# Hybrid decoder layer on one core: the conditioning vector and the first channels' vectors as 11 rows in a transfer of their own

## Chip, cores and metric

The kernel runs on one core of a Trainium2 chip. The metric is the device time of one execution in microseconds (us); lower is better. The time before is the median of three runs.

## What is computed

One decoder layer over 512 tokens and 1024 channels. A conditioning vector `c` yields a shift, a scale and a gate; the normalised input is modulated by shift and scale and goes through one input projection, whose columns feed an attention group and a recurrent group; both are gated, joined and projected back, and a last RMS norm closes the layer. Only the opening concerns the change:

```python
c_act = jax.nn.silu(c)
mod = c_act @ w_mod[l] + b_mod[l]
shift, scale, gate = jnp.split(mod, 3, axis=-1)
h = rmsnorm(x, norm_gain[l]) * (1.0 + scale[:, None, :]) + shift[:, None, :]
proj = h @ w_in[l]
q, k, v, z_attn, x_lru, z_lru = jnp.split(proj, splits, axis=-1)
# attention and RG-LRU groups, each RMS-normed and gated by silu(z)
x = x + gate[:, None, :] * y          # y: both groups through w_out
return rmsnorm(x, final_gain)
```

All of it is in float32.

## The kernel before

Channels lie on the 128 partitions, in eight blocks `d` = 0 to 7 of 128 channels; tokens lie in four tiles `t` of 128. TensorE (PE) computes the products, VectorE (DVE) the sums over weights and the low halves of split operands, ScalarE (ACT) the activations and the high halves; the queue of SyncE (SP) issues nearly all loads. Large products are done three times with operands split into a high and a low part (`split`, line 246), so that they keep float32 accuracy.

**Order of the work.** Every operation is handed to a planner (`Plan`, line 61) with its engine, an assumed cost and a due time. `emit` (line 97) simulates the engines and buffers with these assumed numbers and writes each engine's instructions in the order so found. A changed cost, due time or dependency can therefore move instructions anywhere, and each engine then works through its own list strictly in order.

**The opening.** One table of vectors, `vec` (128 partitions x 80 columns: gains, biases, `c` and others), is loaded from ACT's queue (line 274) beside the four tiles of `x`, which SP loads (line 275). POOL builds the identity matrix `ident`. Then:

- ACT takes silu of the eight columns of `c` into `ccol` (line 317), then loads the table for square roots (line 318). For each token tile it computes the sum of squares and its root (lines 339 and 340), then scales the first 256 channels of tiles 2 and 3 into `xs` (line 348). DVE does that for tiles 0 and 1 (line 351).
- PE spreads `ccol` over all partitions: eight transposes of a column broadcast to 128 x 128, four into each bank `cp` (line 326). DVE copies them into `cb` (line 233).
- DVE multiplies the modulation weights `ws` with `cb` and sums along the row, one sum per channel (line 375 for block 0, line 387 for the others). Then it adds the biases and multiplies by the gain: `g` holds a block's shift (column 0) and its scale (column 1).
- PE turns a block's 128 channels of all four tiles into the bank `xp` (line 407 for block 0, line 403 for the others). ACT makes `h` from `xp` and `g` (line 410), once rounded (`h0h` for block 0) and once in full; DVE subtracts them for the low part. Then PE sums the products of the first seven column blocks into the banks `acc` (line 422).
- Ahead of all that PE has 31 matmuls of 512 columns on a constant tile, `spare` (line 309, `NWARM`), whose result nobody reads. They stand in PE's list between the transposes, where the planner puts them.

After block 7 the rest of the projection, attention, recurrence and output follow, with `vec` read at many places; `spt` (lines 433 to 447) is a small chain on POOL, DVE and ACT that prepares the recurrence's decay, and `halves` (line 476) is half of 20 columns of `vec`.

Of the kernel before, what the change touches and what calls it, by code (L numbers as in the profile page):

```python
# [10 lines left out]
AF = mybir.ActivationFunctionType  # L11
OP = mybir.AluOpType
# [5 lines left out]
ND = D // 128  # L18
# [8 lines left out]
V_GAIN, V_SHIFT, V_SCALE, V_GATE = 0, 8, 16, 24  # L27
V_CW, V_CB, V_BR, V_BI, V_LAM, V_AG, V_LG = 32, 48, 52, 56, 60, 64, 68
V_C = 72
# [31 lines left out]
class Plan:  # L61
# [11 lines left out]
    def op(self, eng, cost, fn, r=(), w=(), due=None, table=None, lat=0.25, after=0.0, alt=None):  # L73
        o = Op(eng, cost, fn, list(r), list(w), due, table, lat, after, alt)
        deps = set()
        for b in o.r:
            if b.writer is not None:
                deps.add(b.writer)
        for b in o.w:
            if b.writer is not None:  # L80
                deps.add(b.writer)
            deps.update(b.readers)
        for b in o.r:
            b.readers.append(o)
        for b in o.w:
            b.writer, b.readers = o, []
        for b in set(o.r) | set(o.w):
            b.users += 1
        deps.discard(o)
        o.deps = list(deps)  # L90
        for d in deps:
            d.outs.append(o)
        o.left = len(deps)
        self.ops.append(o)
        return o
# [80 lines left out]

@with_exitstack
def tile_hymba_block(ctx: ExitStack, tc: tile.TileContext, x, ws0, wss, wgt, win0, wv, winr,
                     wo, wg, vecs, fgain, consts, out):
    nc = tc.nc  # L180
    V, A, G, PE, SP = nc.vector, nc.scalar, nc.gpsimd, nc.tensor, nc.sync
    N2, N4, N8 = 37, 18, 5
# [17 lines left out]
    op = plan.op  # L200
# [4 lines left out]
    def t4(name, dt=F32, shape=(128, 1024)):  # L205
        return Buf("t4", list(shape), dt, name)

    def bank(name, kind=None):
        return Buf("ps", [128, 512], F32, name, kind)

    def col(name):
        return Buf("c", [128, 2], F32, name)

    def fix(name, shape, dt=F32):
        return Buf("fix", list(shape), dt, name)


    def dv(n, ptr=0):
        return 0.075 + n / 960.0 + 0.06 * ptr
# [10 lines left out]
    def copy(n, dst, src, r, w, due=None, psum=False, after=0.0):  # L230

        op("A", acp(n) if psum else ac(n), lambda: A.copy(dst(), src()), r, w, due, after=after,  # L232
           alt=("V", dv(n) if psum else dv2(n), lambda: V.tensor_copy(dst(), src())))
# [4 lines left out]
    def load(dst, src, due, kb=512, queue=SP):  # L238
        op("SP", kb / 390.0, lambda: queue.dma_start(dst[:], src), [], [dst], due, lat=1.9 if due < -98.9 else 2.4 if due < T_REST - 8 else 3.3)
# [21 lines left out]
    def t_first(d):  # L261
        return T_FIRST + 4.79 * d
# [8 lines left out]

    xt = [t4(f"x{t}") for t in range(NT)]
    vec, ident, cst = fix("vec", [128, NV]), fix("ident", [128, 128]), fix("cst", [128, 2048])
    op("A", 0.45, lambda: A.dma_start(vec[:], vecs), [], [vec], -30, lat=1.5)
    for t in range(NT):
        load(xt[t], x[t * 128:(t + 1) * 128, :], -99 + 0.3 * t)
    ws, w0 = {}, {}
    for d in range(ND):
        if d == 0:
            ws[d] = [[Buf("t4" if up - lo > 512 else "t2", [128, up - lo], F32, f"ws0{j}{n}") for n, (lo, up) in enumerate(CUTS[j])] for j in range(2)]  # L280
            for j in (1, 0):
                for n, (lo, up) in enumerate(CUTS[j]):
                    at = 128 * (1024 * j + lo)
                    load(ws[d][j][n], ws0[at:at + 128 * (up - lo)].rearrange("(p n) -> p n", p=128), -97.2 + 0.2 * n - 0.5 * j,
                         kb=(up - lo) / 2)
            w0[d] = [Buf("t2", [128, n], F32, f"w00{n}") for n in (512, 384)]
            load(w0[d][0], win0[d][:, 0:512], -96, kb=256)
            load(w0[d][1], win0[d][:, 512:896], -95, kb=192)
            continue
        w0[d] = t4(f"w0_{d}", F32, (128, 128 * NFIRST))  # L290
        if d < 4:
            ws[d] = [t4(f"ws{d}{j}") for j in range(2)]
            for j in (1, 0):
                load(ws[d][j], wss[d, j], -90 + 3 * (d - 1) - j)
        else:
            b = Buf("t8", [128, 2, 1024], F32, f"ws{d}")
            load(b, wss[d].rearrange("j p n -> p j n"), t_first(d) - 9, kb=1024)
            ws[d] = [b, b]
        load(w0[d], win0[d], t_first(d) - 8.9 if d >= 4 else -92 + 3 * d, kb=448)
# [10 lines left out]
           [warm], [spare], 5.3 + 0.28 * n, lat=0.0)  # L310


    epsc, ones, junk, ccol = fix("epsc", [128, 1]), fix("ones", [128, 1]), fix("junk", [128, 1]), fix("ccol", [128, ND])
    op("V", 0.1, lambda: V.memset(epsc[:], EPS), [], [epsc], -20)
    op("V", 0.1, lambda: V.memset(ones[:], 1.0), [], [ones], 0)
    op("A", 0.1, lambda: A.activation(junk[:], epsc[:], AF.Silu), [epsc], [junk], -6, "silu")
    op("A", 0.1, lambda: A.activation(ccol[:], vec[:, V_C:V_C + ND], AF.Silu), [vec, junk], [ccol], -5, "silu")
    op("A", 0.1, lambda: A.activation(junk[:], epsc[:], AF.Sqrt), [epsc, ccol], [junk], -4, "sqrt")
    cb = t4("cb")
    for half in range(2):  # L320
        ps = bank("cp")
        s = slice(half * 512, (half + 1) * 512)

        def spread(ps=ps, half=half):
            for j in range(4):
                PE.transpose(ps[:, j * 128:(j + 1) * 128], ccol[:, half * 4 + j:half * 4 + j + 1].to_broadcast([128, 128]),  # L326
                             ident[:])
        op("PE", 0.6, spread, [ccol, ident], [ps], 2)
        copy(512, lambda s=s: cb[:, s], lambda ps=ps: ps[:], [ps], [cb], 4.5 + 0.5 * half, True)


# [3 lines left out]
    for t in range(NT):  # L335
# [8 lines left out]
        for dst, cut, e, due2, after in ((xs[t], slice(0, 256), "VVAA"[t], due + 0.4, 0.0), (xt[t], slice(256, D), "A", 20.0 + t, REST[t])):  # L344
            o = (lambda d_, c_: d_[:] if d_ in xs else d_[:, c_])
            n = cut.stop - cut.start
# [3 lines left out]
            else:  # L350
# [6 lines left out]
    hl = [t2(f"h{d}l", F32R) for d in range(ND)]  # L357
    acc = [bank(f"acc{j}") for j in range(NFIRST)]
    op("V", 0.1, lambda: V.tensor_scalar(vec[:, V_SCALE:V_SCALE + ND], vec[:, V_SCALE:V_SCALE + ND], 1.0, None,
                                         op0=OP.add), [vec], [vec], -3)  # L360

    sch = col("sch")

    def part(d, j):
        return ws[d][j][:, j] if d >= 4 else ws[d][j][:]

    def gain(d):

        sc, g = col("sc"), col("g")
        half = (sc, sch)  # L370
        for j in (1, 0):
            if d == 0:
                for n in range(2):
                    lo, up = CUTS[j][n]
                    op("V", dv(up - lo), lambda j=j, n=n, lo=lo, up=up: V.scalar_tensor_tensor(
                        ws[0][j][n][:], ws[0][j][n][:], 1.0, cb[:, lo:up], op0=OP.mult, op1=OP.mult,
                        accum_out=half[n][:, j:j + 1]), [ws[0][j][n], cb], [ws[0][j][n], half[n]], 8 - 2 * j + 0.7 * n)
                    if not n:
                        op("V", 0.1, lambda j=j, v=(V_SHIFT, V_SCALE)[j]: V.tensor_add(
                            sc[:, j:j + 1], sc[:, j:j + 1], vec[:, v:v + 1]), [sc, vec], [sc], 9.2)  # L380
                if j:
                    op("V", 0.2, lambda: V.tensor_scalar(g[:, 1:2], sch[:, 1:2], sc[:, 1:2], vec[:, V_GAIN:V_GAIN + 1],
                                                         op0=OP.add, op1=OP.mult), [sc, sch, vec], [g], 9.4)
                else:
                    op("V", 0.1, lambda: V.tensor_add(g[:, 0:1], sch[:, 0:1], sc[:, 0:1]), [sc, sch], [g], 9.5)
                continue
            op("V", dv(1024), lambda j=j: V.scalar_tensor_tensor(  # L387
                part(d, j), part(d, j), 1.0, cb[:], op0=OP.mult, op1=OP.mult, accum_out=sc[:, j:j + 1]),
               [ws[d][j], cb], [ws[d][j], sc])
        if d == 0:  # L390
            return g
        op("V", 0.2, lambda: V.tensor_scalar(
            g[:, 1:2], sc[:, 1:2], vec[:, V_SCALE + d:V_SCALE + d + 1], vec[:, V_GAIN + d:V_GAIN + d + 1],
            op0=OP.add, op1=OP.mult), [sc, vec], [g])
        op("V", 0.1, lambda: V.tensor_add(g[:, 0:1], sc[:, 0:1], vec[:, V_SHIFT + d:V_SHIFT + d + 1]), [sc, vec], [g])
        return g

    for d in range(ND):
        g, xp = gain(d), bank(f"xp{d}")
# [18 lines left out]
        for i, (a, b) in enumerate(((0, hh[d]), (1, hh[d]), (0, hl[d]))):  # L418
            for j in range(NFIRST):
                w, k = wp[j // 4][a], j if d else j % 4  # L420
# [288 lines left out]
    for u, name in enumerate(UNITS):  # L709
        kind, idx = name[0], int(name[1])  # L710
        t1 = t_step(8 * (u + 1))
        ps = unit(u)
# [41 lines left out]
    for g in range(4):  # L754
        br, half = "la"[g // 2], g % 2
# [5 lines left out]
        for j in range(2):  # L761
            w = t4(f"wo{g}{j}", F32, (128, 2, 512))
# [4 lines left out]
        for t in range(NT):  # L767
# [3 lines left out]
            for n, (lo, up) in enumerate(zip(cuts, cuts[1:])):  # L771
                ps, w = bank("po"), up - lo
# [39 lines left out]
                for to, up, mark in ((outa[t], 512, done_a), (outb[t], 512, done_b))[:1 if last else 2]:  # L812
                    fns = dict(A=lambda t=t, to=to, up=up: A.activation(to[:, :up], to[:, :up], AF.Copy, scale=ssq[t][:, 3:4]),
                               V=lambda t=t, to=to, up=up: V.tensor_scalar(to[:, :up], to[:, :up], ssq[t][:, 3:4], None, op0=OP.mult))
# [86 lines left out]
```

## Time and profile before

| what | value |
|---|---|
| median of three runs | 239.39 us (238.9 to 239.99) |
| profiled execution, its own time | 239.45 us |
| its span, first to last instruction | 237.4 us |
| PE busy | 228.2 us, 96% of the span |
| DVE busy | 201.3 us, 85% |
| ACT busy | 142.2 us, 60% |
| moved by DMA | 38.01 MB, 160 GB/s on average |
| chain that ended last | PE 94%, DMA 2%, ACT 1%, DVE 1% |

The profiled execution lies 0.06 us from the median. About 2.05 us of its time lie outside the span. A busy share is an average over stages; the chain of waits says, stage by stage, which work ended last. In a row of the timeline the first number is the start in us from the beginning of the span, the second how long it lasted; in brackets stands how long the engine had been idle and what released it.

### The profile page before, as it was taken

Reading aid. Unit: us, or ns where it says so; the run is one execution under the profiler, and the core shown is the slowest. Engines: PE = TensorE matmul, PEld = TensorE weight load, DVE = VectorE, ACT = ScalarE, POOL = GpSimd, SP = SyncE. Lnnn points to the kernel's source line nnn. Section 1 sums busy time; section 2 is a strip of 40 time slices with the busy share of each in tenths; the row PEclk is TensorE's granted clock in tenths of the full one; section 3 lists DMA queues with packets and bytes.
Section 4 is the critical chain, followed back from the end, with each engine's and each line's share of the span. In section 5 each row is a group of like instructions: output and inputs, shape, how many; then the busy total and the mean of one; then the engine's idle time right before and its main releaser. Section 6 shows DMA issues by size and latency. Waiting matters only on the chain.

```text
span 237.4 us, 3440 instructions
## 1 busy us (share of the span) xinstructions
PE 228.2 (96%) x1235; PEld 179.3 (76%) x1235; DVE 201.3 (85%) x392; ACT 142.2 (60%) x268; POOL 8.8 (4%) x32
## 2 busy tenths in 40 slices
PE   4999999999999999999999999999999999999990
PEld 2567888888878787884888887878757888888890
DVE  1599998968999898989999989989999999836582
ACT  4989565444477585999992379876475502203263
POOL 1000000017400000000000000000000000000000
PEclk9999999999999999999999999999999999999998
DMA  5999999622232425735502632318502200000044
GB/s 231 410 419 420 416 418 423 279 91 88 88 124 77 155 88 177 260 98 179 171 7 88 239 119 88 109 72 333 197 3 88 88 0 3 0 0 0 0 180 177
DMA packets 11472, 38.01 MB, mean 160 GB/s; under 512 B 1344, under 2 KB 1600, under 8 KB 11328
## 3 DMA queue, kind: packets, MB, share of 16 engines
q1 hardware_dynamic: 11168, 37.49, 42.3%
q10 hardware_dynamic: 288, 0.30, 0.4%
q8 instruction: 10, 0.16, 0.3%
q14 instruction: 6, 0.05, 0.1%
HBM read 35.69 MB, written 2.10 MB: 159 GB/s over the span
## 4 chain that ended last, share of the span: by engine, by line
PE 94%; DMA 2%; ACT 1%; DVE 1%; issue 0%; POOL 0%
PE acc L422 16%; PE pj L242 14%; PE pj L244 13%; PE pj L243 13%; PE po L242 6%; PE po L244 6%; PE po L243 6%; PE av L608 4%; PE sc L566 4%; PE tp L620 4%; PE spare L309 3%; DMA vec<-in_vecs_dram 2%; PE xp L403 1%; PE cp L326 1%; PE ss L744 1%; PE gi L243 0%
## 5 line engine op out<-in xcount | busy, mean ns | idle before, releaser
L582 ACT ACTIVATE z<-z,mn 128x128 f32<-128x128 f32 (+3 forms) x32 | 17.8, 556 | 9.5 <-DVE mn L579 9.5
L387 DVE SCALAR_TENSOR_TENSOR ws<-ws,cb 128x1024 f32<-128x1024 f32 x14 | 16.8, 1219 | 0.0
L579 DVE CUSTOM_DVE_ANT_0 z<-sc,cst 128x128 f32<-128x128 f32 (+3 forms) x32 | 14.6, 485 | 2.1 <-PE sc L566 1.0
L232 ACT COPY pt<-tp 128x128 f32<-128x128 f32 (+3 forms) x29 | 10.5, 413 | 7.9 <-PE tp L620 7.9
L620 PE MATMUL tp<-ident,z 128*128 128x128 f32 x80 | 12.2, 273 | 0.0
L620 PEld LDWEIGHTS tp<-ident,z 128*128 128x128 f32 x80 | 9.8, 140 | 2.5 <-issue 0.2
L793 ACT ACTIVATE o<-xr 128x512 f32<-128x512 f32 x7 | 4.4, 634 | 12.0 <-DVE xr L782 12.0
L782 DVE SCALAR_TENSOR_TENSOR xr<-po,rba,xr 128x512 f32<-128x512 f32 (+2 forms) x9 | 6.2, 691 | 6.2 <-PE po L244 6.0
L309 PE MATMUL spare<-warm 128*128 128x512 bf16 x31 | 9.7, 470 | 1.5 <-DVE warm L307 1.5
L764 DVE TENSOR_TENSOR wo<-wo,grow 128x1024 f32<-128x1024 f32 x8 | 9.7, 1216 | 0.0
L532 DVE SCALAR_TENSOR_TENSOR wgt<-wgt,cb 128x1024 f32<-128x1024 f32 x8 | 9.7, 1216 | 0.0
L608 PE MATMUL av<-pt,v 128*64 128x512 f32 (+3 forms) x64 | 9.5, 439 | 0.0
L593 DVE TENSOR_SCALAR z<-z,sum 128x384 f32<-128x384 f32 (+3 forms) x24 | 8.8, 387 | 0.5
L486 DVE SCALAR_TENSOR_TENSOR xc<-xl,vec,xc 128x511 f32<-128x511 f32 (+2 forms) x12 | 9.0, 746 | 0.1
L608 PEld LDWEIGHTS av<-pt,v 128*64 128x64 f32 x64 | 4.2, 136 | 5.7 <-issue 4.1
L782 DVE SCALAR_TENSOR_TENSOR xr<-po,rbl,xr 128x512 f32<-128x512 f32 x8 | 6.0, 748 | 2.4 <-PE po L244 2.2
L309 PEld LDWEIGHTS <-warm 128*128 128x128 bf16 x31 | 3.5, 117 | 5.9 <-issue 2.5
L642 ACT ACTIVATE sz<-pj 128x512 f32<-128x512 f32 x8 | 4.8, 599 | 4.7 <-PE pj L244 4.1
L410 ACT ACTIVATE h<-xp,g 128x512 f32<-128x512 f32 x8 | 6.2, 772 | 0.0
L643 DVE SCALAR_TENSOR_TENSOR sz<-sz,pj 128x512 f32<-128x512 f32 x8 | 5.4, 679 | 0.8 <-ACT sz L642 0.8
L582 ACT ACTIVATION_READ_ACCUMULATOR z<-z,mn 128x1 f32 x32 | 6.0, 189 | 0.0
L232 ACT CAST wo21h<-wo 128x1024 fp32r<-128x1024 f32 x1 | 1.1, 1052 | 8.0 <-DVE wo L764 8.0
(1119 smaller groups left out, 750.0 us busy)
## 6 DMA issues: line engine op xcount, KB each, us to landing
wc<-in_winr_dram SPq DMA_DIRECT2D x13, 512.0 KB, 4.1
ws<-in_wss_dram SPq DMA_DIRECT2D x4, 1024.0 KB, 11.9
wgt<-in_wgt_dram SPq DMA_DIRECT2D x8, 512.0 KB, 3.3
wo<-in_wo_dram SPq DMA_DIRECT2D x8, 512.0 KB, 3.3
w<-in_win_dram SPq DMA_DIRECT2D x7, 448.0 KB, 9.4
ws<-in_wss_dram SPq DMA_DIRECT2D x6, 512.0 KB, 7.4
x<-in_x_dram SPq DMA_DIRECT2D x4, 512.0 KB, 5.2
wv<-in_wv_dram SPq DMA_DIRECT2D x4, 512.0 KB, 4.3
```

What stands on the lines that cost most here:

```text
L232: op("A", acp(n) if psum else ac(n), lambda: A.copy(dst(), src()), r, w, due, after=after, alt=("V", dv(n) if psum else dv2(n), lambda: V. ...
L242: PE.matmul(ps, lh, rh, start=start, stop=False)
L243: PE.matmul(ps, lh, rl, start=False, stop=False)
L244: PE.matmul(ps, ll, rh, start=False, stop=stop)
L309: op("PE", 0.32 if n < 11 else 0.235, lambda: PE.matmul(spare[:], warm[:, 0:128], warm[:], start=True, stop=True), [warm], [spare], 5.3 + ...
L387: op("V", dv(1024), lambda j=j: V.scalar_tensor_tensor(part(d, j), part(d, j), 1.0, cb[:], op0=OP.mult, op1=OP.mult, accum_out=sc[:, j:j + ...
L422: PE.matmul(acc[j][:], w[:, k * 128:(k + 1) * 128], b[:], start=first, stop=last),
L579: op("V", dv(n) + 0.085, lambda s=s, z=z, mn=mn: V.tensor_tensor_reduce(out=z[:, :n], in0=ps[s][:, cut], in1=cst[:, 2048 - n:2048], op0=OP ...
L582: op("A", ac(n, 1, 1), lambda s=s, z=z, mn=mn, sm=sm: A.activation(z[:, :n], z[:, :n], AF.Exp, bias=mn[:, 0:1], scale=-1.0, accum_out=sm[: ...
L608: PE.matmul(ps2[64 * s:64 * s + 64, k * 128:], vt[k][:, (2 * p + s) * 64:(2 * p + s + 1) * 64], pts[s][:, k, k * 128:], start=(k == 0), st ...
L620: PE.transpose(tp[:, k * 128:(k + 1) * 128], z[:, k * 128:(k + 1) * 128], ident[:])
L782: op("V", dv(w, 1), lambda t=t, ps=ps, c0=c0, c1=c1, br=br: V.scalar_tensor_tensor(res[t][:, c0:c1], ps[:, :c1 - c0], rb[br][:, t:t + 1], ...
```

## The change

The host packs a second table, `top`: 11 rows of 128 values, the eight blocks of `c` and block 0's gain, shift bias and scale bias. ACT's queue now loads `top` into `first` (11 partitions). The large table `vec` is loaded by SP, in the same list as the weights, behind the first of block 1's modulation weights. Silu runs on 8 rows of 128 (`crow`). PE turns the 11 rows into the bank `v0`, of which DVE takes the three vectors of block 0, the scale bias with 1 added. `cb` is filled by eight matmuls of `crow` against a broadcast column of `ident`, in place of eight transposes. Block 0's shift is summed in one instruction rather than two, and the 1 is added to the other scale biases later.

```diff
-    op("A", 0.45, lambda: A.dma_start(vec[:], vecs), [], [vec], -30, lat=1.5)
+    first = fix("first", [11, 128])
+    op("A", 0.2, lambda: A.dma_start(first[:], top), [], [first], -30, lat=1.7)
...
             load(w0[d][1], win0[d][:, 512:896], -95, kb=192)
+            load(vec, vecs, -90.5, kb=64)
...
-    op("A", 0.1, lambda: A.activation(ccol[:], vec[:, V_C:V_C + ND], AF.Silu), [vec, junk], [ccol], -5, "silu")
-    op("A", 0.1, lambda: A.activation(junk[:], epsc[:], AF.Sqrt), [epsc, ccol], [junk], -4, "sqrt")
+    op("A", 0.1, lambda: A.activation(crow[:], first[0:ND, :], AF.Silu), [first, junk], [crow], -5, "silu")
+    op("A", 0.1, lambda: A.activation(junk[:], epsc[:], AF.Sqrt), [epsc, crow], [junk], -4, "sqrt")
+
+
+    ps, v0 = bank("v0"), fix("v0", [128, 3])
+    op("PE", 0.2, lambda ps=ps: PE.transpose(ps[:, 0:11], first[:], ident[0:11, 0:11]), [first, ident], [ps], 1)
+    op("V", 0.2, lambda ps=ps: (V.tensor_copy(v0[:, 0:2], ps[:, ND:ND + 2]), V.tensor_scalar(
+        v0[:, 2:3], ps[:, ND + 2:ND + 3], 1.0, None, op0=OP.add)), [ps], [v0], 2)
...
-                PE.transpose(ps[:, j * 128:(j + 1) * 128], ccol[:, half * 4 + j:half * 4 + j + 1].to_broadcast([128, 128]),
-                             ident[:])
-        op("PE", 0.6, spread, [ccol, ident], [ps], 2)
+                k = half * 4 + j
+                PE.matmul(ps[:, j * 128:(j + 1) * 128], ident[0:ND, k:k + 1].to_broadcast([ND, 128]), crow[:], start=True, stop=True)
+        op("PE", 0.8, spread, [crow, ident], [ps], 2)
...
     op("V", 0.1, lambda: V.tensor_scalar(vec[:, V_SCALE:V_SCALE + ND], vec[:, V_SCALE:V_SCALE + ND], 1.0, None,
-                                         op0=OP.add), [vec], [vec], -3)
+                                         op0=OP.add), [vec], [vec], t_first(1) - 3)
...
-                    op("V", 0.1, lambda: V.tensor_add(g[:, 0:1], sch[:, 0:1], sc[:, 0:1]), [sc, sch], [g], 9.5)
+                    op("V", 0.15, lambda: V.scalar_tensor_tensor(g[:, 0:1], sc[:, 0:1], v0[:, 1:2], sch[:, 0:1],
+                                                                    op0=OP.add, op1=OP.add), [sc, sch, v0], [g], 9.5)
```

Three places show how the lists moved. Line numbers differ by a few between the kernels. The first is PE in the opening, about the spread of `c` (`cp`); ahead of each piece stand spare matmuls alone, five before and four now.

```order
L309 MATMUL spare<-warm 128x512
L326 MATMUL cp<-ident,ccol 128x128 x8
L309 LDWEIGHTS warm
```

```order
L311 MATMUL spare<-warm 128x512
L324 MATMUL v_99<-ident,first 128x11
L335 MATMUL cp<-crow,ident 128x128 x8
L311 LDWEIGHTS warm
```

The turn of the 11 rows is new, and one spare matmul has moved from ahead of `cp` to behind it, so that 27 of the 31 stand behind rather than 26.

The second is DVE in the opening, from its last constant to the first scaled tile.

```order
L315 MEMSET ones 128x1
L359 TENSOR_SCALAR vec<-vec 128x8
L476 TENSOR_SCALAR halves<-vec 128x20
L233 COPY cb<-cp 128x512 x2
L351 RECIPROCAL ss<-ss 128x1
L351 TENSOR_SCALAR xs_131<-x_88,ss 128x256
```

```order
L317 MEMSET ones 128x1
L325 COPY v_107<-v_99 128x2
L325 TENSOR_SCALAR v_107<-v_99 128x1
L233 COPY cb<-cp 128x512 x2
L359 RECIPROCAL ss<-ss 128x1
L359 TENSOR_SCALAR xs_132<-x_88,ss 128x256
```

The two steps on `vec` have left the head of the list, and the two copies out of the turned rows have taken their place.

The third is ACT near block 7, about its rounded activations `h7h` and the exponential's table.

```order
L232 CAST wv0h<-wv_489 128x1024
L410 ACTIVATE h7h<-xp_551,g 128x512
L410 ACTIVATE h_564<-xp_551,g 128x512
L435 ACT_TABLE_LOAD
L435 ACTIVATE spt<-spt 128x4
L232 COPY xl<-acc_235 128x512
```

```order
L232 CAST wv0h<-wv_494 128x1024
L443 ACT_TABLE_LOAD
L443 ACTIVATE spt<-spt 128x4
L418 ACTIVATE h7h<-xp_556,g 128x512
L418 ACTIVATE h_578<-xp_556,g 128x512
L232 COPY xl<-acc_238 128x512
```

The table load and the small step on `spt` now stand ahead of block 7's two activations instead of behind them.

## Rows read from the trace of the kernel before

**Rows 1.** Chain of waits, the opening: start, us, what ended last

```profile
0.79 4.18 DMA vec<-in_vecs_dram
...
5.34 1.94 PE cp L326 x8
...
10.60 1.51 PE spare L309 x7
...
14.63 0.79 ACT h0h L410
```

**Rows 2.** All waits of PE in the span: total us, times, longest

```profile
PE spare L309 <- DVE warm L307: 1.5, 1, 1.5
PE cp L326 <- POOL spt L433: 1.5, 1, 1.5
PE acc L422 <- ACT h0h L410: 0.4, 1, 0.4
```

**Rows 3.** Timeline of PE, 0 to 16 us

```profile
1.54 2.31 PE L309 MATMUL spare<-warm 128*128 128x512 bf16 x5 [1.54 <-DVE warm L307]
5.34 1.94 PE L326 MATMUL cp<-ident,ccol 128*128 128x128 f32 x8 [1.49 <-POOL spt L433]
7.08 3.41 PE L309 MATMUL spare<-warm 128*128 128x512 bf16 x9
...
14.32 0.27 PE L407 MATMUL xp<-ident,xs 128*128 128x128 f32 x1
```

**Rows 4.** Timeline of PE's weight loads, around the rise of the clock

```profile
9.21 0.15 PEld L309 LDWEIGHTS <-warm 128*128 128x128 bf16 x1 [0.28 <-issue]
9.64 0.35 PEld L309 LDWEIGHTS <-warm 128*128 128x128 bf16 x2 [0.28 <-issue]
```

**Rows 5.** Busy time by stretch, 5.34 to 9.64 us; PEclk third from last

```profile
5.34:9.64 4.30, 4.30 (x15) 2.58 (x15) 2.06 (x5) 4.22 (x9) 0.00 (x0) 1.00 1.03 415
```

**Rows 6.** Timeline of ACT, the opening

```profile
4.99 0.21 ACT L317 ACTIVATE ccol<-vec 128x8 f32<-128x8 f32 x1 [2.26 <-DMA vec<-in_vecs_dram]
...
6.62 1.04 ACT L339 ACTIVATE scr<-x 128x1024 f32<-128x1024 f32 x1
```

**Rows 7.** The page's groups of DMA issues: KB each, median us to landing

```profile
wgt<-in_wgt_dram SPq DMA_DIRECT2D x8, 512.0 KB, 3.3
```

**Rows 8.** Tile x up to 12 us, over its four loads from 0.79 us on

```profile
L239 SPq DMA_DIRECT2D x<-in_x_dram x4: 382/420/432, 0.8 to 2.2; - x4
...
DMA to landing us min/median/max: 4.0/5.2/6.4
```

**Rows 9.** The page's count of DMA packets

```profile
DMA packets 11472, 38.01 MB, mean 160 GB/s; under 512 B 1344, under 2 KB 1600, under 8 KB 11328
```

**Rows 10.** Groups by shape, PE's plain float32 products: count, busy us, mean ns

```profile
L608 PE MATMUL av<-pt,v 128*64 128x256 f32 x16 | 2.4, 379 | 0.0
...
L744 PE MATMUL ss<-ones,sq 128*128 128x1 f32 x16 | 1.9, 239 | 0.0
L608 PE MATMUL av<-pt,v 128*64 128x128 f32 x16 | 1.6, 273 | 0.0
```

**Rows 11.** Timeline of DVE, block 0's shift and block 1's second sum

```profile
14.07 0.16 DVE L385 TENSOR_TENSOR g<-sch,sc 128x1 f32<-128x1 f32 x1
...
16.38 1.22 DVE L387 SCALAR_TENSOR_TENSOR ws<-ws,cb 128x1024 f32<-128x1024 f32 x1
```

**Rows 12.** Tile ws, 8 to 9 us: block 1's second load, its issue and landing

```profile
L239 SPq DMA_DIRECT2D ws<-in_wss_dram x1: 328/328/328, 8.6 to 8.6; - x1
...
DMA to landing us min/median/max: 6.2/6.2/6.2
```

**Rows 13.** Timeline of all engines, 36 to 68 us, around block 7

```profile
49.07 0.78 ACT L410 ACTIVATE h7h<-xp,g 128x512 fp32r<-128x512 f32 x1 [2.87 <-PE xp L403]
...
50.55 0.69 DVE L412 TENSOR_TENSOR h7l<-h,h7h 128x512 fp32r<-128x512 f32 x1 [1.75 <-ACT h L410]
...
53.88 0.19 PEld L422 LDWEIGHTS acc<-h7l,w07h 128*128 128x128 f32 x1
```

## What the change does to the time: the prediction

> **What bounds the kernel now.** First the chain of waits over the opening [rows 1]. It begins with the load of `vec`, which lands at 0.79 + 4.18 = 4.97 us, and goes on through silu of `c`, the spread `cp` (5.34 us) and then PE alone: spare matmuls with block 0's four turns between them, to the last of these at 14.32 us [rows 3]. ACT starts `h0h` 0.31 us later, at 14.63 us [rows 1]. Second, all waits of PE [rows 2]: there are three, all before 15.5 us. From the first matmul into `acc` to the end of the projections PE waits for nothing, so what the start of `h0h` gains or loses should reach the end one for one. Third, what holds `h0h`: not only the table of vectors. PE must first get through the 26 spare matmuls that stand behind `cp` in its list, and for these its clock matters. [...] In the row at 9.64 us two weight loads start within 0.35 us [rows 4]: the clock rises at about 9.7 us. Before that PE ran from 1.54 to 3.85 us, stood for 1.49 us, and ran on from 5.34 us [rows 3]. Check of the count: spares start at 7.08 us, six at 0.427 us reach 9.64 us, the other 20 take 4.32 us and three turns 0.33 us (0.11 each, half of an eighth of `cp`): 14.29 us, against 14.32 us in the row.
>
> **Part by part.** The sum is made against the profiled execution (239.45 us), which lies 0.06 us from the median of the runs.
>
> *The small transfer.* Its landing is not in the trace. From below: a later load of 512 KB lands 3.3 us after its issue [rows 7], of which about 1.25 us is moving the data (the four loads of `x`, as large, land from 0.8 + 4.0 = 4.8 to 2.2 + 6.4 = 8.6 us, 1.27 us apart [rows 8]). What is left, 2.05 us, would bring the 11 rows at 2.8 us. From above: `vec`, 4.97 us. The first load of `x`, as large as that later one, needed 4.0 us at the start of the kernel, 0.7 us more [rows 7, 8]. Added to 2.8 this gives 3.5 us, less a little for the 40 KB of `vec` that shared its time. I take 3.4 us.
>
> [...]
>
> *Silu of `c`.* 128 columns rather than 8. The 8 columns take 0.21 us [rows 6]; 120 more at some 0.83 ns (the 1024 columns of `scr` take 1.04 us [rows 6], some 0.19 of it fixed by the 8-column row) add 0.10 us. With 0.14 us to PE's start, as before (5.20 to 5.34 us), `cp` starts at 3.4 + 0.02 + 0.31 + 0.14 = 3.87 us, 1.47 us earlier. The turn of the 11 rows and DVE's two copies run while ACT works and while DVE idles; if they were not hidden they would cost one turn, 0.27 us.
>
> *The spread itself gets longer.* A plain float32 product leaves two records where the source has one (`av`: 32 in the source, 64 records; `ss`: 8 and 16), and each costs 0.106 us more for 128 more columns (379 against 273 ns) [rows 10]: 0.21 us at the fast clock for one product of 128 columns, 0.43 us at the slow one. The eight transposes took 7.08 - 5.34 = 1.74 us [rows 3], one record each; sixteen such records take 3.48 us. So `cp` ends at 7.35 us at the slow clock, 0.27 us later than before, and the 1.47 us are spent. If the clock rises in between, what is left of `cp` costs half.
>
> *One spare more behind `cp`:* 27, so 0.22 us at the fast clock. Ahead of `cp` four remain, from 1.54 to 3.25 us, and PE's stop shrinks from 1.49 us to some 0.2 before the turn and 0.2 before `cp`.
>
> *What then decides is when the clock rises.* Every microsecond by which it rises earlier saves half a microsecond of spares and spread. With the rise at time W after `cp`, the last turn starts at W + 0.216 x (27 - (W - 7.35)/0.427) + 0.33. The rows give two ends. If the rise moves with the start of `cp`, it comes at 9.7 - 1.47 = 8.2 us: last turn 13.95 us, a gain of 0.37. If the short stops no longer count and it moves as if the work began at 1.54 us instead of 5.34 us, it comes at 9.7 - 3.8 = 5.9 us: 2.03 us of `cp` slow, the other 1.45 at half, end 6.63, then 5.83 + 0.33: 12.79 us, a gain of 1.53. No row is nearer to one end, so I take the middle, 7.05 us: 3.18 us slow, the other 0.30 at half, end 7.20, last turn 13.36 us, a gain of **0.95 us**.
>
> *Other engines.* ACT's sums of squares start 1.42 us after silu's end before (5.20 to 6.62) [rows 6]; now at 3.73 + 1.42 = 5.15 us, 1.47 earlier; the tiles of `x`, landed from 4.8 to 8.6 us [rows 8], don't hold them (the fourth would start at 9.25). DVE has `g` at 14.23 us before [rows 11]; 1.47 earlier and one instruction of 0.16 less is 12.6. So `h0h` can't start before 12.7 us: a gain of 1.93 is the ceiling.
>
> *`vec` in SP's list* costs an issue of about 0.33 us and 40 KB, some 0.1 us of the queue; the same bytes leave the stretch before. Behind it waits block 1's second modulation load, landed at 8.6 + 6.2 = 14.8 us [rows 12] and used at 16.38 us [rows 11]: 1.6 us of cover, 0.6 with the gain of 0.95. Cost nothing; with the cover gone, up to 0.4 us. The added 1 on `vec` (0.17 us) moves into DVE's busy stretch ahead of block 1's `g`, behind which ACT is busy with a tile of `x`: nothing.
>
> *Block 7.* The table load (1.28 us) and `spt`'s step now precede `h7h`. ACT is idle for 2.87 us just there [rows 13]: hidden; without cover 1.5 us. DVE's `h7l` goes behind two steps on `wv1`, to some 52 us; PE needs it at 53.88 us [rows 13]: hidden.
>
> Sum: 239.4 - 0.95 = **238.4 us**.
>
> **Rivals.**
> 1. *The spares stop being the bound.* The clock rises early in `cp`, at 5.0 us: 1.13 us slow, the other 2.35 at half, last turn at 12.34 us, and `g` sets the start, 12.7 us. Gain 1.9: **237.5 us**. For it: only two short stops are left after 1.54 us. Against: before, the rise came only well behind `cp`.
> 2. *The rise stays at 9.7 us.* Then 5.5 spares are slow and 21.5 fast: 14.67 us, 0.35 later: **239.7 us**. For it: nothing but one execution ties the rise to the work. Against: before, it came in the midst of unbroken work.
> 3. *The slower side: the eight-row products don't wake the clock.* They fill 8 of 128 partitions. If the rise follows the spares behind `cp` as it followed `cp` before, it comes 7.35 - 5.34 = 2.0 us later, at 11.7 us: 10.2 spares slow, 16.8 fast, 15.66 us, 1.34 later: **240.7 us**. It decides as soon as the rise is later than 9.0 us, where the formula gives the 14.32 us of before. Against it: the rows call PE busy for any product.
> 4. *The change doesn't do what it says:* the 11 rows land with the first tile of `x`, at 4.8 us. `cp` runs from 5.27 to 8.75 us; with the rise at 9.6 us two spares are slow and 25 fast: 15.33 us, 1.0 later: **240.4 us**. [...]
>
> **How the numbers follow.** Forecast 0.42, rival 1 0.25, rival 2 0.18, rival 3 0.10, rival 4 0.05. The range runs from rival 1 (237.5) up to just short of rival 3, 240.5 us; it holds the forecast's own 237.9 to 239.0 and rivals 1, 2 and 4 and leaves out rival 3 and parts of the edges. About 0.5%, 1.2 us, is what a measurement of this kernel can tell from no change. Faster by more than that: rival 1, less a little, and the quarter of the forecast with the rise before 6.5 us, 0.36. Slower by more: half of rival 3, part of rival 4 and of rival 2 with a late rise, 0.11. The rest, 0.53.
>
> **What would show it.** `first` landing at 3.2 to 3.7 us; 16 records of `cp` starting near 3.9 us; the spacing of spares dropping from 0.43 to 0.22 us between 5.9 and 8.2 us; the last turn near 13.4 and `h0h` near 13.7 us; `acc` from about 14.5 us without a wait; no wait of PE around block 7. The forecast is wrong if the spacing drops after 9 us, if `first` lands after 4 us, or if PE, which now never waits after 15.5 us, waits for `h1h` or a weight load.

## The result: slower, and where the time went

| | before | after |
|---|---|---|
| median, six runs each, same chip | 239.61 us (238.9 to 240.35) | 241.07 us (240.27 to 241.36) |
| ratio of after to before | | 1.0064 (95% interval 1.0048 to 1.0081) |
| profiled execution, its own time | 239.45 us | 240.82 us |
| its span | 237.4 us | 238.5 us |
| outside the span | 2.05 us | 2.32 us |

The forecast was 238.4 us with a range of 237.5 to 240.5; the median rose by 1.46 us (1.37 us in the profiled pair) and lies above the range. The chain of waits of after, over the opening (start, us, what ended last):

```profile
1.54 1.89 PE spare L311 x4
3.42 0.21 PE v L324
3.63 3.61 PE cp L335 x16
7.24 3.53 PE spare L311 x8
10.77 0.21 PE xp L415
10.98 1.82 PE spare L311 x7
12.80 0.11 PE xp L415
12.91 1.94 PE spare L311 x9
...
15.76 0.79 ACT h0h L418
...
16.59 5.05 PE acc L430 x21
```

Where before began with the load of `vec` [rows 1], no transfer stands here any more: the chain is PE from 1.54 us until `h0h`. So the change did what it says. And yet `h0h` starts at 15.76 us, 1.13 us later than the 14.63 us of [rows 1]. The eight spares behind `cp` take 3.53 us, 0.44 us each. The timeline of PE, then of its weight loads, in after:

```profile
1.54 1.89 PE L311 MATMUL spare<-warm 128*128 128x512 bf16 x4 [1.54 <-DVE warm L309]
3.35 0.28 PE L324 MATMUL v<-ident,first 11*128 11x11 f32 x1
3.48 3.76 PE L335 MATMUL cp<-crow,ident 8*128 8x128 f32 x16
7.17 3.59 PE L311 MATMUL spare<-warm 128*128 128x512 bf16 x8
...
14.80 0.81 PE L311 MATMUL spare<-warm 128*128 128x512 bf16 x3
15.45 0.27 PE L415 MATMUL xp<-ident,xs 128*128 128x128 f32 x1
```

```profile
9.28 0.15 PEld L311 LDWEIGHTS <-warm 128*128 128x128 bf16 x1 [0.28 <-issue]
9.71 0.15 PEld L311 LDWEIGHTS <-warm 128*128 128x128 bf16 x1 [0.28 <-issue]
...
10.56 0.36 PEld L311 LDWEIGHTS <-warm 128*128 128x128 bf16 x2 [0.20 <-issue]
11.20 0.15 PEld L311 LDWEIGHTS <-warm 128*128 128x128 bf16 x1 [0.28 <-issue]
11.56 0.75 PEld L311 LDWEIGHTS <-warm 128*128 128x128 bf16 x4 [0.21 <-issue]
```

One spare still follows another at 0.43 us (9.28 to 9.71 us, and again at 11.20); only from 11.56 us on do four weight loads start within 0.75 us, and nine spares pass in 1.94 us, 0.216 each. Before, the same step came at 9.64 us [rows 4]. The clock thus rises at about 11.5 us, 1.8 us later than before, though the profile shows no wait of PE from 1.54 us to the first product of `acc`. As before [rows 5], the granted clock reads 1.00 in the slow stretch too. So what is called the rise of the clock here is a step in the pace of PE, told by the spacing (0.43 to 0.216 us) and not by the granted clock. The fields after the comma are PE, PEld, DVE, ACT and POOL busy, then PEclk, DMA share and GB/s:

```profile
7.17:10.50 3.33, 3.33 (x9) 1.26 (x9) 2.39 (x9) 2.69 (x7) 0.00 (x0) 1.00 1.03 394
```

Behind `h0h` PE waits no more than before. These are all waits of PE in after, against those of [rows 2]:

```profile
PE spare L311 <- DVE warm L309: 1.5, 1, 1.5
PE acc L430 <- ACT h0h L418: 0.4, 1, 0.4
```

The wait ahead of `cp` is gone, and PE waits for nothing later. So the 1.13 us at `h0h` reach the end as 1.1 us of span; another 0.27 us lie outside the span.

### The profile page after: what moved, and what is told of

Read it like the earlier page. It is cut to its first block, busy times and chain, and to the rows that moved or that the text cites. A ratio compares the mean times of both kernels' runs of the same rounds, so it can differ in the third digit from the quotient of the medians.

```text
span 238.5 us, 3458 instructions
## 1 busy us (share of the span) xinstructions
PE 230.9 (97%) x1244; PEld 181.4 (76%) x1244; DVE 201.4 (84%) x393; ACT 142.3 (60%) x268; POOL 9.5 (4%) x32
## 4 chain that ended last, share of the span: by engine, by line
PE 96%; ACT 1%; DVE 1%; issue 0%
PE acc L430 16%; PE pj L242 14%; PE pj L244 13%; PE pj L243 13%; PE po L242 6%; PE po L244 6%; PE po L243 6%; PE spare L311 4%; PE av L616 4%; PE sc L574 4%; PE tp L628 4%; PE cp L335 2%; PE xp L411 1%; PE ss L752 1%; PE gi L244 0%; PE gr L242 0%
## 5 line engine op out<-in xcount | busy, mean ns | idle before, releaser
L628 PE MATMUL tp<-ident,z 128*128 128x128 f32 x80 | 12.2, 273 | 0.0
L311 PE MATMUL spare<-warm 128*128 128x512 bf16 x31 | 10.3, 489 | 1.5 <-DVE warm L309 1.5
```

Source lines behind the costliest of these rows:

```text
L311: op("PE", 0.32 if n < 11 else 0.235, lambda: PE.matmul(spare[:], warm[:, 0:128], warm[:], start=True, stop=True), [warm], [spare], 5.3 + ...
L628: PE.transpose(tp[:, k * 128:(k + 1) * 128], z[:, k * 128:(k + 1) * 128], ident[:])
```

## Experiments

Two theories stood first. **A:** products that contract over 8 partitions don't bring the clock up (rival 3). **B:** it is not their shape but their place or length, or a clock that rises late for another reason (rival 2).

**e1: the same products over all partitions.** The added 120 rows of `crow` are zeros, so the result and the count of columns stay; only the partitions taken change. (The edits below are shown shortened.)

```diff
-crow = fix("crow", [ND, 128])
+crow = fix("crow", [128, 128])
+V.memset(crow[:], 0.0)
-A.activation(crow[:], first[0:ND, :], AF.Silu)
+A.activation(crow[0:ND, :], first[0:ND, :], AF.Silu)
-PE.matmul(..., ident[0:ND, k:k + 1].to_broadcast([ND, 128]), crow[:], ...)
+PE.matmul(..., ident[:, k:k + 1].to_broadcast([128, 128]), crow[:], ...)
```

> The changed kernel, but the eight products that spread c run over all 128 partitions: crow is 128 rows, 120 of them zero. Number, width and type of the records stay as they are. Theory A (the clock does not rise on products of eight rows; it rises only behind work on all partitions): 'spare' drops from 0.43 to 0.22 us spacing at 6 to 8.5 us instead of 11.5, the last turn starts near 13.5 instead of 15.45, time about 239.1 us. Theory B (the rise comes when it comes; the loss is the longer spread and the spare moved behind it): no change, 241.0 us.

Measured: 238.52 us, ratio to before 0.9969 (0.9954 to 0.9985), where after has 1.0064: some 2.3 us less than after, and 0.6 us under what A had put. The timeline of PE and its weight loads in e1:

```profile
3.71 3.78 PE L336 MATMUL cp<-crow,ident 128*128 128x128 f32 x16
...
7.71 0.15 PEld L311 LDWEIGHTS <-warm 128*128 128x128 bf16 x1 [0.28 <-issue]
8.13 0.75 PEld L311 LDWEIGHTS <-warm 128*128 128x128 bf16 x4 [0.28 <-issue]
...
13.65 0.27 PE L416 MATMUL xp<-ident,xs 128*128 128x128 f32 x1
```

`cp` takes as long as in after (3.78 against 3.76 us), and it is 128*128 in place of 8*128; the spacing drops at 8.13 us, not at 11.5. This is A. In PE's list up to the rise nothing but the partitions differs from after. Further back the planner moved one of the 27 spares behind the last turn, which is 0.22 us of the gain; in the profiled pair `h0h` starts 1.80 us earlier (13.96 against 15.76 us).

**e2: the small transfer kept, the spread as before,** with `c` taken as eight columns from the turned 11 rows and eight transposes.

```diff
-PE.matmul(..., ident[0:ND, k:k + 1].to_broadcast([ND, 128]), crow[:], ...)
+A.activation(ccol[:], ps[:, 0:ND], AF.Silu)      # ps: the bank of the turned rows
+PE.transpose(..., ccol[:, k:k + 1].to_broadcast([128, 128]), ident[:])
```

> The changed kernel with the small transfer, but c spread as in the kernel before: the turned rows give c as columns, silu runs on eight columns, eight transposes of a broadcast column fill cb. Eight records instead of sixteen, all partitions. Theory A: cp from about 4.1 to 5.9 us, rise near 8 us, last turn near 12.7, then g (13.1 us) sets h0h: about 238.1 us. Theory B with the rise at 11.5 us: last turn near 14.4 us, 239.7 us.

Measured: 238.6 us, 0.997 (0.9956 to 0.9984). A fits the clock better than the time. In e2:

```profile
4.47 1.91 PE L335 MATMUL cp<-ident,ccol 128*128 128x128 f32 x8
...
6.61 1.19 PEld L311 LDWEIGHTS <-warm 128*128 128x128 bf16 x6 [0.28 <-issue]
...
12.25 0.33 PE L415 MATMUL xp<-ident,xs 128*128 128x128 f32 x1
...
13.28 0.22 DVE L392 SCALAR_TENSOR_TENSOR g<-sc,v,sch 128x1 f32<-128x1 f32 x1
...
13.60 0.78 ACT L418 ACTIVATE h0h<-xp,g 128x512 fp32r<-128x512 f32 x1
```

The clock is up at 6.6 us and the last turn goes at 12.25 us, 1.35 us before `h0h`. The spares are no longer the bound: `g` is, which ends at 13.50 us here, 0.91 us later than in e1. Silu stands behind the turn of the rows in this kernel, so that ACT's first sum of squares starts 0.35 us later than in e1 (5.35 against 5.00 us); the third starts some 0.15 us late on top of that, as its tile of `x` lands (8.2 us); and DVE waits 0.31 us for a part of block 0's modulation weights. That is the ceiling of the prediction, reached later than the 12.7 us put there.

**e3: the kernel before with eight-row spares.** The same cause, put where the change isn't.

```diff
-PE.matmul(spare[:], warm[:, 0:128], warm[:], start=True, stop=True)
+PE.matmul(spare[:], warm[0:8, 0:128], warm[0:8, :], start=True, stop=True)
```

> The kernel before, but the 31 spare matmuls contract over 8 partitions instead of 128; same columns, same order. Theory A: the clock does not rise while they run; 26 of them at 0.43 us bring the last turn to about 18.9 us, and the first sums into acc run slowly as well: 244 to 246 us. Theory B: as before, 239.6 us.

Measured once: 246.38 us, with the last turn at 19.62 us, both somewhat beyond what A had put (246 and 18.9). The timeline of PE in e3:

```profile
6.88 4.02 PE L309 MATMUL spare<-warm 8*128 8x512 bf16 x9
...
14.73 4.02 PE L309 MATMUL spare<-warm 8*128 8x512 bf16 x9
...
20.96 2.07 PE L422 MATMUL acc<-h0h,w00512h 128*128 128x512 f32 x4
...
24.11 1.25 PE L422 MATMUL acc<-h0h,w00512l 128*128 128x512 f32 x4
25.21 0.85 PE L422 MATMUL acc<-h0h,w00384l 128*128 128x512 f32 x3
```

All 31 spares stay at the slow spacing (nine in 4.02 us; the nine of [rows 3], six of them slow, take 3.41), and the first four products of `acc` take 2.07 us against 1.19 us in a kernel with the clock up (e4). PE was busy from 5.01 us on, and the clock rose only at about 24.5 us, some 3.5 us into the products of `acc`, which take all partitions (four take 1.25 us from 24.11 on, the next three 0.85). B has no place for this: nothing but the partitions of the spares was changed.

**e4: after with 20 spares** (`NWARM = 31` to `20`), so that the slow clock has less to slow down.

> The changed kernel with 20 spare matmuls instead of 31, 16 of them behind the spread. Both theories: if the spares are what holds h0h, the last turn comes 11 x 0.216 = 2.4 us sooner, near 13.1 us, level with g; h0h near 13.4, time about 238.7 us. If something else holds h0h (DVE's g, a load), no change, 241.0 us.

Measured: 238.69 us, 0.997 (0.9952 to 0.9987), as expected. The clock rises no earlier than in after (spacing 0.43 us until 12.16), but the last two turns go at 13.38 us. So what the late clock costs hangs on the spares that stand in PE's list ahead of the last turn. It is not all gone: `g` ends at 13.30 us, and ACT still waits for PE.

```profile
13.79 0.78 ACT L418 ACTIVATE h0h<-xp,g 128x512 fp32r<-128x512 f32 x1 [0.53 <-PE xp L415]
```

**What is the small transfer worth, when the spares hold up nothing?** e4 leaves open whether before gains by fewer spares too, and whether the gain of e1 grows.

**f1**, the kernel before with 20 spares:

> The kernel before with 20 spare products in place of 31; nothing else is changed, and the computation is whole. Theory A (in the kernel before two things end together: the row of spares with the last turn at 14.32 us and the column g, whose last step ends at 14.23): h0h waits for g, starts at 14.2 to 14.3 in place of about 14.6, and the time falls by 0.3 to 0.4 us, to 238.8. Theory B (the spares are the whole bound, and g comes earlier too once ScalarE and VectorE are not waiting for TensorE): h0h starts near 13.3 and the time is 237.9.

**f2**, e1 with 20 spares:

> The kernel after with the eight products over all 128 partitions (as in e1_full_rows) and 20 spare products in place of 31. Theory A (with the clock up at 8 us and no spare behind the last turn's operands, what is left is the column g, which ended at 12.6 us in e1_full_rows): the last turn goes by 12.3, h0h starts at 12.6 to 12.9 in place of 13.96, the span is 235.4 to 235.8 and the time 237.2 to 237.6. Theory B (with the spares thinned out the engine stops between the turns, the clock falls or rises later, and the first accumulations run slow): no better than e1_full_rows, 238.5.

Measured: f1 238.86 us, 0.9997 (0.9978 to 1.0015); f2 238.09 us, 0.9977 (0.9949 to 1.0005). In their profiled executions `h0h` waits for `g`, as the theories A have it: f1 starts it at 13.95 us, right behind `g` (13.69 + 0.16 us), and f2 at 12.83 us. f1 is some 0.3 us ahead of what was expected, and not by its spares: `vec` landed earlier than in the profiled execution of before, where silu of `c` starts at 4.99 us [rows 6].

```profile
4.62 0.21 ACT L317 ACTIVATE ccol<-vec 128x8 f32<-128x8 f32 x1 [1.91 <-DMA vec<-in_vecs_dram]
```

f2's span (235.6 us) is what A had put, but 2.4 us lie outside it, so that even this execution, at 238.03 us, is above A's 237.2 to 237.6. And the intervals are wide, since both kernels have executions 1 us and more longer: three of ten of f1 lie at 240.1 to 240.2 and seven at 238.8 to 238.9; of f2 eight lie at 237.8 to 238.2 and four at 239.1 to 241.2. For those four, B's time is the nearer one.

f4 (f2 with the transfer padded to 16 rows, of which more below) has two such executions in twelve, and its profile is one of them. The mean granted clock goes with it: in the nine longer executions of f1, f2 and f4 it is 0.980 to 0.990, in the other 25 it is 0.991 to 0.998. PE at the first products of `acc`, f4 and then f2:

```profile
13.95 1.88 PE L431 MATMUL acc<-h0h,w00512h 128*128 128x512 f32 x4 [1.34 <-ACT h0h L419]
15.63 1.48 PE L431 MATMUL acc<-h0h,w00384h 128*128 128x512 f32 x3
```

```profile
13.66 1.19 PE L431 MATMUL acc<-h0h,w00512h 128*128 128x512 f32 x4 [1.34 <-ACT h0h L419]
14.69 0.85 PE L431 MATMUL acc<-h0h,w00384h 128*128 128x512 f32 x3
```

Busy time of f4 by stretch, PEclk third from last: the wait, and then three stretches behind it.

```profile
12.61:13.95 1.34, 0.00 (x1) 0.00 (x0) 1.30 (x5) 0.83 (x2) 0.33 (x1) 1.00 1.06 418
13.95:14.20 0.25, 0.25 (x1) 0.25 (x2) 0.25 (x1) 0.25 (x1) 0.00 (x0) 1.00 0.98 391
14.30:17.50 3.20, 3.20 (x9) 2.47 (x8) 3.12 (x10) 3.20 (x5) 0.00 (x0) 0.50 1.02 419
17.70:20.00 2.30, 2.30 (x12) 1.89 (x11) 2.30 (x4) 2.30 (x4) 0.00 (x0) 1.00 1.03 423
```

Both kernels wait 1.34 us ahead of `acc`, and PE's list before that is the same, its times alike to some 0.3 us. In f4 the granted clock is still 1.00 in the wait and falls to 0.50 between 14.2 and 14.3 us, some 0.3 us after PE has begun on `acc`, to read 1.00 again from 17.7 us on; in f2 the same seven products go at 1.19 and 0.85 us, and the mean granted clock of the execution is 0.995 against f4's 0.990. Whether the spares that cost time ahead of the last turn would earn it behind, where PE waits, was tried next:

```diff
+for n in range(6):        # behind block 0's last turn
+    op("PE", 0.235, lambda: PE.matmul(spare[:], warm[:, 0:128], warm[:], start=True, stop=True),
+       [warm, xp], [spare], 9, lat=0.0)
```

**g1**, f4 with six spares more in the wait:

> f4_full_16_20 with six spare products more, which stand behind the last turn, where TensorE otherwise waits some 1.4 us for h0h; so 26 spares in all, none of which the last turn has to wait for. Theory A (that wait, and nothing in the loads, is what makes some executions of the kernels with 20 spares 1.2 us longer: the clock falls in it, and the first accumulations run at half speed): h0h still starts at 12.8 to 13.2, no execution is 1 us above the others, and the time is 238.0 or less. Theory B (the longer executions come from elsewhere): one execution in four or five is still 1.2 us longer.

**g2**, f1 with the same six:

> f1_before_20 with the same six spare products behind the last turn: the kernel before with its spares where they hold up nothing, and so what is left when the small transfer isn't there. Theory A (as for g1_full_16_fill): all executions at 238.8, none at 240.1; h0h at 13.95 as in f1_before_20, by the column g. The distance to g1_full_16_fill is then what the small transfer itself is worth: 0.6 to 1.0 us. Theory B: still some executions at 240.1.

Measured: g1 238.26 us, 0.9962 (0.9947 to 0.9976), seven executions between 238.11 and 238.47; g2 238.88 us, 0.9987 (0.9975 to 0.9999), its twelve spans all 236.7 or 236.8 us (two of its times, 239.19 and 239.72, are longer by what lies outside the span). In both the executions with 1.2 us more of span are gone: none of 28 has one, with those of g3 below, where f1, f2 and f4 have nine of 34. The loads are those of f4 and f1, so it isn't they. But that the wait by itself does it is not shown: e2 waits 1.41 us ahead of `acc`, behind 31 spares, and none of its ten executions is longer. g1's time lies 0.26 us above what A had put. In g1 PE, `g` and `h0h` read:

```profile
11.41 0.73 PE L416 MATMUL xp<-ident,xs 128*128 128x128 f32 x2 [0.44 <-ACT xs L357]
...
11.97 1.46 PE L419 MATMUL spare<-warm 128*128 128x512 bf16 x6
...
12.78 0.22 DVE L393 SCALAR_TENSOR_TENSOR g<-sc,v,sch 128x1 f32<-128x1 f32 x1
...
13.09 0.78 ACT L421 ACTIVATE h0h<-xp,g 128x512 fp32r<-128x512 f32 x1 [0.83 <-DVE g L393]
```

`h0h` now waits for `g` alone. With its spares out of the way the small transfer is worth 238.88 - 238.26 = 0.62 us (0.53 us with 11 rows, g3): some 1.0 us of span (medians 236.8 and 235.8), less some 0.3 us outside it (2.07 and 2.36).

**Eleven rows or sixteen.** In after the four tiles of `x` land 3.3 to 7.0 us after their issue, the third and fourth late (before: 4.0 to 6.4 [rows 8]). Do 11 rows ahead of them make these loads uneven? (The edit is shown shortened.)

```diff
-first = fix("first", [11, 128])
+first = fix("first", [16, 128])
-top = vecs.T[[c0..c7, gain, shift, scale]]
+top = vecs.T[[c0..c7, gain, shift, scale, c0..c4]]
```

**f3**, e1 with 16 rows, the five added ones read by nobody; **f4**, f2 with 16 rows; **g3**, g1 with 11 rows:

> [...] Theory A (the 11 rows fall on 11 of 16 engines and make the loads behind them land unevenly): the four x tiles land at even steps of 0.8 us as in the kernel before (4.0, 4.8, 5.6, 6.4 us from their issue), and the last of them by 6.4. Theory B (the unevenness has nothing to do with the count of rows): the third and fourth still land at 6.2 or later in some run like this one. The time by both is 238.5, since the spares stand in front of the last turn.

> f2_full_20 with the small transfer padded to 16 rows. Theory A (uneven landings cost the loads of the first scale vectors some 0.3 to 0.6 us, and with the spares thinned out these are what h0h waits for): 0.2 to 0.5 us under f2_full_20, some 237.0. Theory B (they don't): the same as f2_full_20.

> g1_full_16_fill with the small transfer of 11 rows as in the kernel after. Theory A (16 rows in place of 11 make the loads behind land evenly, and the column g hangs on them): 0.2 to 0.5 us slower than g1_full_16_fill, with the last x tile at 7 us in some of its executions. Theory B (the count of rows does nothing to the time): within 0.15 us of g1_full_16_fill.

The last tile of `x` landed, with 11 rows ahead of it, at 7.0 (after), 6.1 (e1), 7.3 (e2), 7.2 (e4), 6.1 (f2) and 6.9 us (g3); with 16 rows at 5.9 (f3), 6.0 (f4) and 6.0 us (g1). With 11 rows, ACT waited 0.3 to 0.6 us for a tile of `x` in after and e4, and DVE 0.2 to 0.5 us for modulation weights in after, e2, e4 and g3; in the three with 16 rows, and in the kernels where `vec` goes first, neither waited. That speaks for A, by one execution each, as far as the landings go: over which engines the rows go is shown by no run, and stays the author's conjecture. And with 11 rows e1 and f2 land as early as the kernels with `vec` first. But the padded rows themselves come later: silu starts at 3.66 to 3.70 us in the three with 16 rows, at 2.83 to 3.40 in after, e1, e4, f2 and g3. In time nothing is left: f3 238.55 us against e1's 238.52, f4 238.26 against f2's 238.09, g1 238.26 against g3's 238.35 (0.9963, 0.9951 to 0.9975). B holds for the time.

**g4: the transfer by itself,** added to the kernel before and read by nobody.

> The kernel before with the small transfer of 11 rows added behind that of the table of vectors, into a tile that nobody reads: the cost of one more transfer and one more input by itself. Theory A (it costs what stands outside the span: 2.25 to 2.4 us there in the kernels with it, 2.12 in the kernel before): the time outside the span rises to 2.25 or more, the span stays, and the time is 239.3 to 239.4. Theory B (what stands outside the span hangs on something else): 2.12 us outside the span, and the time is 239.1.

Measured: 239.04 us, 0.9995 (0.9983 to 1.0006). Outside the span lie 2.31 us (median of ten) against 2.11 us in the 27 runs of before beside it; the span has not grown (medians 236.75 and 237.0). So half of what was expected came: the 0.2 us are the transfer's or the added input's, which of the two stays open, and the sum came out under 239.3 because the span was a little shorter than that of before. (The planner put one more spare ahead of `cp`, six in place of five, where PE waits anyway.)

## Why the prediction was wrong, step by step

| kernel | spread over | clock up at | last turn | `g` ends | `h0h` starts | span |
|---|---|---|---|---|---|---|
| before | 128 partitions | 9.7 | 14.32 | 14.23 | 14.63 | 237.4 |
| after | 8 | 11.5 | 15.45 | 13.11 | 15.76 | 238.5 |
| e4 | 8 | 12.2 | 13.5 | 13.30 | 13.79 | 236.5 |
| e1 | 128 | 8.1 | 13.65 | 12.59 | 13.96 | 236.7 |
| f3 | 128 | 5.2 | 12.40 | 12.99 | 13.08 | 235.8 |
| e2 | 128 | 6.6 | 12.25 | 13.50 | 13.60 | 236.7 |
| g1 | 128 | 6.6 | 11.9 | 13.00 | 13.09 | 235.9 |

(us, one profiled execution each. Within `cp` the rise is an estimate from its length: a record follows another in 0.231 us at the slow clock, 3.69 us for sixteen in after, and is taken to need half of that at the fast one, as the spares do, 0.216 for 0.43 us. The last turn of e4 and g1 is the second of a pair, at 13.38 and 11.41 us.)

**The landing was mis-sized, on the good side.** `first` was put at 3.4 us. Silu of it starts at 2.83 us without a wait for a transfer, so in after it had landed by then, within 2.05 us of its issue: the lower bound, not the value near the upper. In other runs silu still waited for it (e1 until 3.27 us, f3 until 3.66 us), so the bounds were right, and 3.4 was no bad value. The landing that it was set against was less typical: in the profiled execution of before silu of `c` starts at 4.99 us, in the four others with the same opening (e3, f1, g2, g4) at 4.62 to 4.70 us. So some 0.3 of the 1.47 us that the small transfer was to bring belong to that one execution.

```profile
0.78 0.62 ACTq L275 DMA_DIRECT2D first<-in_top_dram  x1
...
2.83 0.29 ACT L319 ACTIVATE crow<-first 8x128 f32<-8x128 f32 x1
```

Rival 4 falls with this: the rows came 1.3 us ahead of the first tile of `x`, which landed at 4.1 us (3.3 us after its issue), although the two loads were issued within 0.01 us of each other (0.78 and 0.79 us).

**The length of `cp` was right in its count:** sixteen records. They took 3.69 us (3.48 to the first spare at 7.17) where 3.48 was forecast, and began 0.39 us earlier, so that they ended at 7.17 us where 7.20 stood. That the ends agree is luck: the 7.20 had the clock rise within `cp`.

**The count of spares was right,** 27 (8 + 7 + 9 + 3 in the timeline), and so was the formula. Its two spacings are measured: 0.427 us (six spares from 7.08 to 9.64 us [rows 3, 4]) and 0.216 us (seven in 1.51 us [rows 1]); after has 0.43 us (9.28 to 9.71 us) and 0.216 us (nine in 1.94 us). With the rise that was measured, 11.5 us, and the start at 7.17 us it gives 11.5 + 0.216 x (27 - 4.33/0.427) + 0.33 = 15.47 us; the last turn stands at 15.45. For e1, with 26 spares, 7.28 and 8.13 us, it gives 13.65 us; measured 13.65.

**The step that failed is the place of the clock's rise.** The prediction took the middle of 5.9 and 8.2 us, both worked out as if `cp` counted like any other work ("if the rise moves with the start of `cp`", "if the short stops no longer count"). It rose at 11.5 us in after and at 12.2 us in e4, behind eight-row products, past the 9 us that the prediction itself named as the sign of being wrong. With the spread over all partitions it rose between 5.2 and 8.1 us in the seven profiled kernels with the small transfer, in four of them (f3, f4, g1, g3) within `cp`; for such a spread the two ends were well put, though f3 and g3 lie under the lower one. With the opening of before it rose at 8.5 us (g2) to 10.2 us (g4); so in none of eleven profiled kernels without eight-row products does its scatter reach 11.5 us. In f3, where sixteen records take 2.44 us to the first spare, five of them are slow by the same estimate:

```profile
4.02 2.61 PE L336 MATMUL cp<-crow,ident 128*128 128x128 f32 x16
6.46 1.68 PE L311 MATMUL spare<-warm 128*128 128x512 bf16 x7
```

That `cp` would be another kind of work for the clock stood in the text only as rival 3, with 11.7 us, a last turn at 15.66 and 240.7 us: the outcome that came, with its numbers, at a chance of 0.10. What was said against it, that the rows call PE busy for any product, is no evidence: in e3 PE is busy for 10.0 of 10.0 us at the slow spacing.

```profile
5.00:15.00 10.00, 9.99 (x27) 4.04 (x28) 6.84 (x22) 8.01 (x17) 0.00 (x0) 1.00 1.03 413
```

Up to the rise, e1 and after differ in PE's work in the partitions alone, and the spacing drops at 8.13 us in the one and at 11.5 us in the other.

**The outside of the span was not in the sum.** It grew by 0.27 us in the profiled pair, and by 0.2 us for the transfer alone (g4). Had it been there, rival 3 would have stood at 240.9 us, beside the 240.82 of the profiled execution.

**The other engines were read rightly, but for the tiles of `x`.** `g` ends at 13.11 us, 1.1 us earlier than before, and lies ready for 2.6 us while ACT waits for PE. That is 0.5 us later than the 12.6 put, though silu ran 0.6 us earlier than put: the tiles of `x` did hold ACT's sums, by 0.57 us at the third, and DVE waited 0.20 us for a part of block 0's modulation weights. With PE the bound it cost nothing here. Block 1's second modulation load was used at 17.44 us without a wait. Block 7 came through: `h7h` starts at 50.26 and `h7l` at 52.49 us, and the products there run on.

```profile
50.26 0.78 ACT L418 ACTIVATE h7h<-xp,g 128x512 fp32r<-128x512 f32 x1 [0.64 <-PE xp L411]
...
52.49 0.68 DVE L420 TENSOR_TENSOR h7l<-h,h7h 128x512 fp32r<-128x512 f32 x1
```

**Rivals 1 and 2.** Rival 1 (the spares no longer the bound, 237.5 us) is what e2, f3, f2 and g1 come near in their profiled executions, once the spread takes all partitions (f2 and g1 with fewer spares too): `h0h` waits for `g`, in 235.6 to 236.7 us of span. Their times, 238.1 to 238.6 us, stay above it. Rival 2 (the rise stays at 9.7 us) did not come, but its warning was right, that one execution is little to tie the rise to the work.

## What to carry to other kernels

Where a stretch is paced by PE's products, as here up to the last turn, ask of every replaced product not only how long it takes but whether the spacing still drops behind it. Products over 8 partitions cost as much time as full ones (sixteen of `cp`: 3.76 and 3.78 us), but the clock rose at 11.5 us with them in `cp` (after) and at 24.5 us with them as spares (e3), against 8.1 us with full ones (e1); zero rows up to 128 cost one memset and gave back some 2.3 us. Nothing between 8 and 128 partitions was measured. And six spares more did no harm where PE would wait anyway (g1 238.26 us as f4, g2 238.88 against f1's 238.86), while eleven of the same products ahead of the last turn held it up (13.38 us in e4, 15.45 in after).

## What was not expected of the hardware

- With eight-row spares the spacing stayed slow through their whole stretch, from 6.88 to 19.6 us (nine in 4.02 us at its start and again from 14.73 us on), and on to about 24.5 us, although PE was busy without a stop from 5.01 us (e3). For the eight-row products of `cp`, zero rows were enough: the spacing dropped at 8.1 us (e1) in place of 11.5 us (after).
- The rise scatters between executions of kernels whose PE work is alike up to it: 8.1 us in e1 and f2, 5.2 us in g3 (the last by the estimate within `cp`). A single profile gives the clock's place to some 3 us only.
- After a wait of the same length, 1.34 us, the granted clock fell to 0.50 in one execution (f4), some 0.3 us after PE had started again, and the first four products of `acc` took 1.88 us; in another (f2) they took 1.19 us; nine of 34 executions with such a wait (f1, f2, f4) were about 1 us or more longer, and none of 28 once six products filled it (g1, g2, g3).
